# The opening of a 1-core decoder layer: turning x before its norm is known

## The chip, the cores and the metric

The kernel runs on one core of a Trainium2 chip. The metric is the device time in microseconds (us) of one execution. A time is the median of several executions; beside it stands one execution that the hardware profiler recorded, from which all durations of single instructions come.

The engines are called as the profile calls them: PE is TensorE's matrix product and PEld its weight load, DVE is VectorE, ACT is ScalarE, POOL is GpSimd, SP is SyncE, which here only issues DMAs.

## The reference

One layer of a decoder over 512 tokens of width 1024, all in float32. Cut to what the opening of the kernel computes:

```python
def rmsnorm(x, g):
    y = x * rsqrt(mean(x * x, axis=-1) + 1e-6)
    return y * g

u = rmsnorm(x, ln1_g)                 # x [512, 1024]
proj = u @ w_in                       # q, k, v, pool_in, z, xbc, dt, gates
# pooling branch: for each of 4 groups of 256 columns of pool_in, window w in (2, 4, 8, 16)
#   d = (sum of the last w tokens) / min(t + 1, w) - pool_in
#   y_b = concat(d @ pool_w[group]) * pool_scale @ w_b
```

After it come attention of three dilations, a state-space branch, gates, an output projection, a gated convolutional feed-forward block and a final norm. They are not touched.

## The kernel before

**Precision.** A float32 product is made of three products of a shorter format: a matrix a is split into a high part `ah` (rounded to the short format) and a low part `al = a - ah`, and `a @ b` is taken as `ah @ bh + ah @ bl + al @ bh`. For weights, `cast` makes `wh` on ACT (L195) and `lows` makes `wl` on DVE or POOL (L215). For the normed, transposed x the parts lie in `uh` and `ul`, [128, 8, 512]: 128 rows of the width, 8 steps k of it, 512 tokens.

**Jobs.** The work is a list of jobs, each with a block of weights (mostly 1024 x 256, 1 MB) and a body of matrix products. The loop at the end runs the bodies one after the other; before each it issues the low part of the next block, the cast of the one after, and the load of the third. Raw blocks have two buffers. The order on PE, ACT, DVE and POOL is the order in which the program is written (a manual schedule); only SP's queue is not part of it. PSUM has eight banks: four of the tag `mm` for products and four of the tag `sm` for short uses, transposes among them.

**The opening.** The first two jobs (columns 0 to 511 of `pool_in`, pooling groups 0 and 1) are written out by hand ahead of the loop, since the norm of x must be made first. x comes as four blocks of 128 tokens, each in two halves of 512 columns (`xin[tb, h]`). While it loads, PE multiplies ones (`warm_up`, L1493). For blocks 0 and 1 the squares are summed on ACT and DVE, the factor r = 1/sqrt(mean + eps) is made by a chain of short DVE instructions around a square root on ACT, and put on a diagonal matrix `diag`. PE multiplies each 128 x 128 piece of x by `diag` (`turn_scale`, L1552): this transposes and scales at once, into the four `sm` banks, where bank `k % 4` holds the 256 tokens of step k and of step k + 4. `turned` then reads each result, multiplies it by the norm's weight `g1` and splits it: `uh` on ACT (L1522), `ul` on DVE (L1523).

`begin(n, lo, hi)` makes the products of job n for tokens lo to hi into the `mm` banks `first[2n]` and `first[2n+1]` (all L1535): first, interleaved by k, `wh` with `uh` and `ul` (32 products of 256 columns), then `wl` with `uh` (16). The order on PE is

```python
    begin(0, 0, 256)
    begin(1, 0, 256, turns)   # turns: after its first 32 products, transpose blocks 2 and 3
    turn()                    # one transpose of small columns ("colp"), into an sm bank
    begin(0, 256, S)
    begin(1, 256, S)
```

Blocks 2 and 3 are scaled by their factors in place (`xin`, L1587 on DVE and L1589 on ACT), after a chain of its own (`rstd_of`, L421 to L430), and are transposed by plain transposes (L1600). Where all 512 tokens of a bank are done, `pool_evac` copies the bank to `u` (L775) and starts the windowed sums on POOL. The loop's first job is the third block of weights (its products carry L234).

Of the kernel before, what the change touches and what calls it, by code (L numbers as in the profile page):

```python
# [10 lines left out]
F32 = mybir.dt.float32  # L11
# [5 lines left out]
P = 128  # L17
# [66 lines left out]
def trunk(ctx: ExitStack, tc, out, x, rel_bias, ln1_g, w_in, b_gate, w_a, pool_w, pool_scale, w_b,  # L84
# [23 lines left out]
    def T(name, dt=F32, shape=(P, S)):  # L108
        return big.tile(list(shape), dt, name=name, tag="t")
# [76 lines left out]
    def cast(job, cuts=1, spread=False):  # L186

        w = job.c // cuts
        if job.form:
            job.raw = job.form()  # L190
        job.high = whp.tile([P, job.k, job.c], F32R, name="wh", tag="wh")

        def high(i):
            o = slice(i * w, (i + 1) * w)
            act.copy(job.high[:, :, o], job.raw[:, :, o])  # L195
# [12 lines left out]
    def lows(job, cuts=1, eng=None):  # L208

        w, h = job.c // cuts, job.high  # L210
        l = wlp.tile([P, job.k, job.c], F32R, name="wl", tag="wl")
        job.split = h, l
        for i in range(cuts):
            o = slice(i * w, (i + 1) * w)
            (eng or dve).tensor_tensor(l[:, :, o], job.raw[:, :, o], h[:, :, o].bitcast(F32),  # L215
                                       OP.subtract)
# [216 lines left out]
    def squares(eng, src, ss):  # L433
        junk = T("junk")
        if eng is act:
            act.activation(junk, src, AF.Square, accum_out=ss)
        else:
            dve.scalar_tensor_tensor(junk, src, 1.0, src, OP.mult, OP.mult, accum_out=ss)
# [328 lines left out]

    ramp = cpool.tile([P, 4, 16], F32, name="ramp")
    DP, YB = {}, {}

    def pool_evac(m, ps):
        g = m // 2
        w = 2 << g
        u = T("pu")
        act.copy(u, ps)  # L775
        cur, sh = u, 1
        while sh < w:
            nxt = T("psw")
            pool.tensor_tensor(nxt[:, sh:], cur[:, sh:], cur[:, :S - sh], OP.add)
            pool.tensor_copy(nxt[:, :sh], cur[:, :sh])  # L780
            cur, sh = nxt, sh * 2
        pool.tensor_tensor(cur[:, :w], cur[:, :w], ramp[:, g, :w], OP.mult)

        def later():
            yield
            yield
            d = T("pd")
            dve.scalar_tensor_tensor(d, cur, 1.0 / w, u, OP.mult, OP.subtract)
            dh, dl = T("pdh", F32R), T("pdl", F32R)
            act.copy(dh, d)  # L790
            dve.tensor_sub(dl, d, dh.bitcast(F32))
            DP[m] = (dh, dl)

        running.append(later())
# [690 lines left out]
    act.dma_start(g8[:KD, :P], ln1_g[0].rearrange("(k p) -> k p", p=P))  # L1485
    dve.memset(ones, 1.0)
    dve.memset(warm, 1.0)
# [3 lines left out]
    def warm_up(n):  # L1491
        for i in range(n):
            pe.matmul(first[3][:, :P], ones, ones, start=True, stop=True)  # L1493

    fetch(weights[0], 2)
    fetch(weights[1])
    load_x(2)
    load_x(3)
# [17 lines left out]
    def x_block(tb, k):  # L1516
        return xin[tb, k // 4][:, (k % 4) * P:(k % 4 + 1) * P]

    def turned(k, lo, ps):

        hh = uh[:, k, lo:lo + 256]
        act.mul(hh, ps, g1[:, k:k + 1])  # L1522
        dve.scalar_tensor_tensor(ul[:, k, lo:lo + 256], ps, g1[:, k:k + 1], hh.bitcast(F32),  # L1523
                                 OP.mult, OP.subtract)

    def begin(n, lo, hi, between=lambda early: None):
        wh, wl = weights[n].split
        order = [(wh, uh, 0)]
        for k in range(1, KD):
            order += [(wh, uh, k), (wh, ul, k - 1)]  # L1530
        order.append((wh, ul, KD - 1))
        for part in (order, [(wl, uh, k) for k in range(KD)]):
            for a, b, k in part:
                for j in range(2):
                    pe.matmul(first[2 * n + j][:, lo:hi], a[:, k, j * P:(j + 1) * P], b[:, k, lo:hi],  # L1535
                              start=a is wh and b is uh and k == 0, stop=a is wl and k == KD - 1)
            between(part is order)
        if hi == S:
            for j in range(2):
                pool_evac(2 * n + j, first[2 * n + j])  # L1540
                step()


    warm_up(WARM)
    diag = [T("diag") for _ in range(2)]
    banks = [SM("uT") for _ in range(4)]

    def bank(k):
        return banks[k % 4][:, (k // 4) * 256:(k // 4) * 256 + 256]

    def turn_scale(tb, k):
        pe.matmul(bank(k)[:, tb * P:(tb + 1) * P], x_block(tb, k), diag[tb][:, :P], start=True, stop=True)  # L1552

    for tb in range(2):
        s0, s1, v, sq, r, rt = (small(n, [P, 1]) for n in ("s0", "s1", "v", "sq", "r", "rt"))
        squares(act, xin[tb, 0], s0)
        squares((dve, act)[tb], xin[tb, 1], s1)
        dve.tensor_scalar(v, s0, 1.0 / D, EPS, OP.mult, OP.add)
        dve.scalar_tensor_tensor(v, s1, 1.0 / D, v, OP.mult, OP.add)
        act.activation(sq, v, AF.Sqrt)  # L1560
        dve.reciprocal(r, sq)
        dve.scalar_tensor_tensor(rt, r, v, r, OP.mult, OP.mult)
        dve.tensor_scalar(rt, rt, -0.5, 1.5, OP.mult, OP.add)
        dve.tensor_scalar(diag[tb][:, :P], eye, r, rt, OP.mult, OP.mult)
        if tb == 0:
            for k in range(KD):
                turn_scale(0, k)
    pe.transpose(first[2][:, :KD], g8[:KD, :P], eye[:KD, :KD])
    dve.tensor_copy(g1, first[2][:, :KD])
    cast(weights[0], 2)  # L1570
    low(weights[0], 2, pool)
    for k in range(KD):
        turn_scale(1, k % 2 * 4 + k // 2)
    for k in range(KD):
        turned(k, 0, bank(k))
    cast(weights[1], 2)
    parts = lows(weights[1], 2)


    ss = row_squares(2, small("ss", [P, 4]), 2)  # L1580
    next(parts)
    r = rstd_of(ss, 2, D)
    for tb in (2, 3):
        for h in range(2):
            t = xin[tb, h]
            if h:
                dve.tensor_scalar(t, t, r[:, tb - 2:tb - 1], None, OP.mult)  # L1587
            else:
                act.mul(t, t, r[:, tb - 2:tb - 1])  # L1589
    next(parts)  # L1590
    begin(0, 0, 256)

    def turns(early):
        if not early:
            return
        for k in range(4):
            banks[k] = SM("uT")
        for k in range(KD):
            for tb in range(2):
                pe.transpose(bank(k)[:, tb * P:(tb + 1) * P], x_block(2 + tb, k), eye)  # L1600
        for k in range(KD):
            turned(k, 256, bank(k))

    begin(1, 0, 256, turns)
# [6 lines left out]
    begin(1, 256, S)  # L1611
    cast(weights[3])
    fetch(weights[4])

# [68 lines left out]
```

## Time and profile before

| | us |
|---|---|
| median of 3 runs | 1043.03 |
| lowest and highest | 1042.78, 1044.10 |
| the profiled execution | 1044.23 |
| its span, first to last instruction | 1042.4 |

A row of the timeline gives the start and the length in us, the engine, the line, the operation, what it writes and reads, the shape, how many instructions were merged, and in brackets the idle time before with what ended it. A matrix product's length is modelled and overlaps the next one; the distance between starts is what counts. A row of the groups gives the shape, the count, the busy time in us and the mean length of one in ns, and the idle time before. In a row of windows the granted clock of TensorE is a share of full speed.

### The profile page before, as it was taken

The numbers are of one execution on the slowest core, as the hardware profiler recorded it, in microseconds if no ns is written. First come the engines' busy times: TensorE is split into PE (matmuls) and PEld (weight loads), VectorE is DVE, ScalarE is ACT, GpSimd is POOL, SyncE is SP. The second block draws the span as 40 slices with busy tenths as digits, with TensorE's granted clock in tenths as the row PEclk, the third lists the DMA queues.
The fourth block names the chain that finished last, engine by engine and source line by source line (L and its number), as shares of the span: only waits on it lengthen the run. The fifth ranks groups of instructions, "written<-read, shape, count | busy, mean of one in ns | idle before, by whom it ended". The sixth has DMA issues, their size and how long they took to land.

```text
span 1042.4 us, 13096 instructions
## 1 busy us (share of the span) xinstructions
PE 1030.2 (99%) x5214; PEld 864.4 (83%) x5214; DVE 645.8 (62%) x864; ACT 466.9 (45%) x756; POOL 151.1 (14%) x125
## 2 busy tenths in 40 slices
PE   8999999999999999999999999999999999999997
PEld 8988878898888878888888888898888888878885
DVE  5563566684356658766768666767766566556645
ACT  5432554452464364557545233544444344433331
POOL 1680000000000004210152500002111111110110
PEclk9999999999999999999999999999999999999999
DMA  8345222126222344552243326642232322362332
GB/s 294 107 116 148 97 66 75 31 62 201 81 81 81 98 135 112 142 137 80 68 132 122 121 81 242 220 162 86 87 116 81 121 81 97 105 242 70 112 101 81
DMA packets 119788, 121.81 MB, mean 117 GB/s; under 512 B 5523, under 2 KB 101590, under 8 KB 119727
## 3 DMA queue, kind: packets, MB, share of 16 engines
q1 hardware_dynamic: 119135, 120.12, 36.4%
q8 instruction: 41, 0.67, 0.3%
q10 hardware_dynamic: 592, 0.86, 0.2%
q14 instruction: 20, 0.16, 0.1%
HBM read 115.07 MB, written 4.32 MB: 115 GB/s over the span
## 4 chain that ended last, share of the span: by engine, by line
PE 97%; DVE 1%; ACT 1%; DMA 0%; issue 0%; DVEq 0%; SPq 0%; ACTq 0%
PE pa L234 35%; PE pu L234 22%; PE pb L234 17%; PE pqk L234 9%; PE pa L1535 2%; PE p L234 2%; PE ps L662 1%; PE pu L1356 1%; PE ppw L234 1%; PE pt L690 1%; PE po L703 1%; PE py L988 1%; PE uT L1552 1%; PE pyo L995 1%; PE pst L974 0%; DMA xin<-in_x_dram 0%
## 5 line engine op out<-in xcount | busy, mean ns | idle before, releaser
L215 DVE TENSOR_TENSOR wl<-raw,wh 128x2048 fp32r<-128x2048 f32 (+3 forms) x95 | 217.1, 2287 | 73.9 <-ACT wh L195 41.7
L195 ACT CAST wh<-raw 128x1024 fp32r<-128x1024 f32 (+3 forms) x188 | 189.5, 1026 | 63.0 <-DVE raw L337 21.1
L234 PE MATMUL pa<-uh,wh 128*128 128x512 f32 x384 | 98.5, 398 | 0.0
L1192 DVE SCALAR_TENSOR_TENSOR hc<-pu,fcol,hc 128x510 f32<-128x510 f32 x88 | 65.8, 748 | 51.1 <-ACT hc L1189 49.5
L234 PE MATMUL pa<-ul,wh 128*128 128x512 f32 x384 | 94.9, 389 | 0.0
L234 PE MATMUL pa<-uh,wl 128*128 128x512 f32 x384 | 94.9, 389 | 0.0
L234 PEld LDWEIGHTS pa<-ul,wh 128*128 128x128 f32 x384 | 72.1, 188 | 15.2
L234 PEld LDWEIGHTS pa<-uh,wl 128*128 128x128 f32 x384 | 72.1, 188 | 15.0
L234 PE MATMUL pu<-uh,wh 128*128 128x512 f32 (+1 forms) x352 | 83.7, 380 | 0.0
L234 PE MATMUL pu<-ul,wh 128*128 128x512 f32 (+1 forms) x352 | 83.5, 379 | 0.0
L234 PE MATMUL pu<-uh,wl 128*128 128x512 f32 (+1 forms) x352 | 83.5, 379 | 0.0
L234 PEld LDWEIGHTS pa<-uh,wh 128*128 128x128 f32 x384 | 70.3, 188 | 14.7 <-issue 1.0
L234 PEld LDWEIGHTS pu<-uh,wh 128*128 128x128 f32 x352 | 64.1, 188 | 12.6 <-ACT uh L452 0.2
L234 PEld LDWEIGHTS pu<-ul,wh 128*128 128x128 f32 x352 | 64.2, 188 | 12.5
L234 PEld LDWEIGHTS pu<-uh,wl 128*128 128x128 f32 x352 | 64.2, 188 | 12.5
L1189 ACT ACTIVATE hc<-pu,fcol,fcol 128x512 f32<-128x512 f32 x40 | 31.2, 780 | 75.6 <-PE pu L234 75.4
L1197 POOL TENSOR_TENSOR hc<-hc 128x512 f32<-128x512 f32 x22 | 31.5, 1431 | 223.5 <-DVE hc L1192 169.3
L950 POOL TENSOR_TENSOR xd<-xc,dec 128x512 f32<-128x512 f32 x6 | 6.4, 1061 | 333.7 <-DVE xc L944 314.8
L1077 ACT ACTIVATE sg<-pa,col 128x512 f32<-128x512 f32 x24 | 16.5, 688 | 55.5 <-PE pa L234 48.7
L683 ACT ACTIVATE sb<-sb,both 128x128 f32<-128x128 f32 (+1 forms) x72 | 30.1, 419 | 23.5 <-DVE both L680 13.4
L234 PE MATMUL pqk<-uh,wh 128*128 128x512 f32 x144 | 36.9, 394 | 0.0
L234 PE MATMUL pqk<-ul,wh 128*128 128x512 f32 x144 | 36.3, 389 | 0.0
(355 smaller groups left out, 1765.1 us busy)
## 6 DMA issues: line engine op xcount, KB each, us to landing
raw<-in_w_in_dram SPq DMA_DIRECT2D x25, 1024.0 KB
raw<-in_ffn_w_up_dram SPq DMA_DIRECT2D x22, 1024.0 KB
raw<-in_w_in_dram SPq DMA_DIRECT2D x20, 512.0 KB
raw<-in_ffn_w_down_dram SPq DMA_DIRECT2D x10, 1024.0 KB
raw<-in_w_o_dram SPq DMA_DIRECT2D x8, 1024.0 KB
raw<-in_w_b_dram SPq DMA_DIRECT2D x4, 1024.0 KB
al<-ad SPq DMA_DIRECT2D x16, 256.0 KB
raw<-in_w_c_dram SPq DMA_DIRECT2D x4, 1024.0 KB
```

The lines of the kernel that those rows point to most:

```text
L195: act.copy(job.high[:, :, o], job.raw[:, :, o])
L215: (eng or dve).tensor_tensor(l[:, :, o], job.raw[:, :, o], h[:, :, o].bitcast(F32), OP.subtract)
L234: pe.matmul(ps, l, r, start=first and n == 0, stop=last and n == total - 1)
L662: pe.matmul(pss[i][:, o:o + w * P], q[r, n * P:(n + 1) * P], k[r, kb * P:(kb + w) * P], start=True, stop=True)
L683: act.activation(sb[:, off:off + w * P], sb[:, off:off + w * P], AF.Exp, bias=nm[:, n, h:h + 1], accum_out=ls[:, n, h:h + 1])
L690: pe.transpose(pt[:, o:o + P], sb[:, o:o + P], eye)
L703: pe.matmul(po[DH * hh:DH * hh + DH, n * P:(n + 1) * P], V[g, kb + i][:, (2 * cc + hh) * DH:(2 * cc + hh + 1) * DH], probs[2 * cc + hh, mb ...
L1077: act.activation(s, ps, AF.Sigmoid, bias=col[:, o:o + 1])
L1189: act.activation(t, ps, AF.Identity, bias=ff["c1"][:, ff["b"] + m:ff["b"] + m + 1], scale=fw(2, m))
L1192: dve.scalar_tensor_tensor(t[:, sh:], ps[:, :S - sh], fw(k, m), t[:, sh:], OP.mult, OP.add)
L1197: pool.tensor_tensor(a, a, t, OP.mult)
L1535: pe.matmul(first[2 * n + j][:, lo:hi], a[:, k, j * P:(j + 1) * P], b[:, k, lo:hi], start=a is wh and b is uh and k == 0, stop=a is wl and ...
```

## The change

For the first 256 tokens the norm's factor is taken out of the way of the products.

- Blocks 0 and 1 of x are transposed as they are (`turned` is now this transpose), into the same four `sm` banks, `lo`. Between them stand the transpose of the norm's weight and a further warm-up, and another one behind.
- `scaled` multiplies by `g1` and splits into new tiles: `rh` on ACT, `rl` on DVE. Job 0's and job 1's products of these tokens (`highs`, then `lows_of`) run on `rh` and `rl`, with no factor. Since the factor belongs to a token, that is to a column of the result, it is applied to the result: `pool_evac` of the first four banks multiplies the first 256 columns by `rb` on DVE.
- `rb` is the row of factors on all partitions: a diagonal `dg` made on DVE, multiplied by ones on PE (`spread`, in the middle of job 1's high products), copied from the bank by ACT.
- The other jobs still need normed `uh` and `ul` for these tokens. They are made out of the banks: DVE multiplies each `lo[k]` by `g1` and `rb` into `un`; ACT copies that into `uh`, DVE subtracts it into `ul`, during the second half. The chain for blocks 2 and 3 and their scaling stand between the fourth and the fifth of DVE's eight passes. Only then do the `sm` banks take the transposes of blocks 2 and 3.
- Job 0's weights are loaded and split in halves by k instead of by columns; the first half's `wh` is a copy on DVE, the second's a copy on ACT. Job 1's `wl` is made on POOL instead of DVE. The identity matrix `eye` is loaded ahead of block 1 of x.

```diff
     def pool_evac(m, ps):
...
-        act.copy(u, ps)
+        if m < 4:
+            dve.tensor_tensor(u[:, LO], ps[:, LO], rb[0], OP.mult)
+            act.copy(u[:, HI], ps[:, HI])
+        else:
+            act.copy(u, ps)
...
     load_x(0)
+    act.dma_start(eye, c_eye)
     load_x(1, act)
-    act.dma_start(eye, c_eye)
     act.dma_start(g8[:KD, :P], ln1_g[0].rearrange("(k p) -> k p", p=P))
...
-    fetch(weights[0], 2)
+    w0 = weights[0]
+    w0.raw = wraw.tile([P, KD, 256], F32, name="raw", tag="raw")
+    HALF = (slice(0, 4), slice(4, 8))
+    for ks in HALF:
+        sp.dma_start(w0.raw[:, ks, :], w0.parts[0][:, ks, :])
...
+    def scaled(oh, ol, k, ps):
+        act.mul(oh, ps, g1[:, k:k + 1])
+        dve.scalar_tensor_tensor(ol, ps, g1[:, k:k + 1], oh.bitcast(F32), OP.mult, OP.subtract)
+
+    def highs(n, A, B, o, between=None):
+        wh, order = weights[n].split[0], [(A, 0)]
         for k in range(1, KD):
+            order += [(A, k), (B, k - 1)]
+        order.append((B, KD - 1))
+        for i, (m, k) in enumerate(order):
+            if between and i == KD:
+                between()
             for j in range(2):
+                pe.matmul(first[2 * n + j][:, o], wh[:, k, j * P:(j + 1) * P], m(k),
+                          start=m is A and k == 0, stop=False)
+
+    def lows_of(n, A, o):
+        for k in range(KD):
+            for j in range(2):
+                pe.matmul(first[2 * n + j][:, o], weights[n].split[1][:, k, j * P:(j + 1) * P], A(k),
+                          start=False, stop=k == KD - 1)
...
+    def turned(tb, k, ps):
+        pe.transpose(ps[:, tb % 2 * P:(tb % 2 + 1) * P], x_block(tb, k), eye)
...
     warm_up(WARM)
+    lo = banks_of_two()
+    for k in range(KD):
+        turned(0, k, lo[k])
     pe.transpose(first[2][:, :KD], g8[:KD, :P], eye[:KD, :KD])
     dve.tensor_copy(g1, first[2][:, :KD])
+    warm_up(3)
     for k in range(KD):
+        turned(1, k, lo[k])
+    warm_up(6)
+    ss = small("ss", [P, 8])
+    for h in range(2):
+        squares(act, xin[0, h], ss[:, 4 * h:4 * h + 1])
...
+    def split0(ks, copy):
+        copy(w0.high[:, ks, :], w0.raw[:, ks, :])
+        pool.tensor_tensor(wl[:, ks, :], w0.raw[:, ks, :], w0.high[:, ks, :].bitcast(F32), OP.subtract)
+
     for k in range(KD):
+        if k == 1:
+            split0(HALF[0], dve.tensor_copy)
+        if k == 5:
+            split0(HALF[1], act.copy)
+        scaled(rh(k), rl(k), k, lo[k])
+    highs(0, rh, rl, LO)
+    squares(act, xin[1, 0], ss[:, 1:2])
+    squares(dve, xin[1, 1], ss[:, 5:6])
+    dve.tensor_tensor(ss[:, :2], ss[:, :2], ss[:, 4:6], OP.add)
+    r = rstd_of(ss[:, :2], 2, D)
+    dg = T("dg")
+    dve.tensor_tensor(dg[:, LO].rearrange("p (b t) -> p b t", b=2), eye.unsqueeze(1).to_broadcast([P, 2, P]),
+                      r.unsqueeze(2).to_broadcast([P, 2, P]), OP.mult)
+    lows_of(0, rh, LO)
     cast(weights[1], 2)
+    low(weights[1], 2, pool)
+
+    def spread():
+        pe.matmul(first[0][:, HI], ones, dg[:, LO], start=True, stop=True)
+        rb.append(T("rb")[:, :256])
+        act.copy(rb[0], first[0][:, HI])
+
+    ss2 = row_squares(2, small("ss2", [P, 4]), 2)
+    highs(1, rh, rl, LO, spread)
+    us = []
+    for k in range(KD):
+        if k % 2 == 0:
+            us.append(T("un"))
+        t = us[-1][:, k % 2 * 256:k % 2 * 256 + 256]
+        dve.scalar_tensor_tensor(t, lo[k], g1[:, k:k + 1], rb[0], OP.mult, OP.mult)
+        if k == 3:
+            r = rstd_of(ss2, 2, D)
+            for tb in (2, 3):
+                for h in range(2):
+                    t = xin[tb, h]
+                    if h:
+                        dve.tensor_scalar(t, t, r[:, tb - 2:tb - 1], None, OP.mult)
+                    else:
+                        act.mul(t, t, r[:, tb - 2:tb - 1])
+    hi = banks_of_two()
+    for k in range(KD):
+        for tb in (2, 3):
+            turned(tb, k, hi[k])
+    lows_of(1, rh, LO)
+    for k in range(KD):
+        scaled(uhi(k), uli(k), k, hi[k])
+    for i, t in enumerate(us):
+        act.copy(uh[:, 2 * i:2 * i + 2, LO], t.rearrange("p (k t) -> p k t", k=2))
     turn()
     fetch(weights[2])
     fetch(weights[3])
-    begin(0, 256, S)
+    highs(0, uhi, uli, HI)
+    for i, t in enumerate(us):
+        dve.tensor_sub(ul[:, 2 * i:2 * i + 2, LO], t.rearrange("p (k t) -> p k t", k=2),
+                       uh[:, 2 * i:2 * i + 2, LO].bitcast(F32))
+    lows_of(0, uhi, HI)
...
```

More of the change, by code (lines that the diff above doesn't have):

```diff
@@ L769, in trunk @@
     DP, YB = {}, {}
+    rb = []
     def pool_evac(m, ps):
@@ L1517, in x_block @@
         return xin[tb, k // 4][:, (k % 4) * P:(k % 4 + 1) * P]
[L1519 to L1528, printed above, removed]
-        for k in range(1, KD):
[L1530 to L1538, printed above, removed]
-            for j in range(2):
-                pool_evac(2 * n + j, first[2 * n + j])
-                step()
@@ L1544, in trunk @@
-    warm_up(WARM)
[L1545 to L1567, printed above, removed]
+    def scaled(oh, ol, k, ps):
+        act.mul(oh, ps, g1[:, k:k + 1])
+        dve.scalar_tensor_tensor(ol, ps, g1[:, k:k + 1], oh.bitcast(F32), OP.mult, OP.subtract)
@@ new lines, in trunk, with rh, rl, uhi @@
+    raws = [T("rh", F32R) for _ in range(8)]
+    def rh(k):
+        return raws[k // 2][:, k % 2 * 256:k % 2 * 256 + 256]
+    def rl(k):
+        return raws[4 + k // 2][:, k % 2 * 256:k % 2 * 256 + 256]
+    def uhi(k):
+        return uh[:, k, HI]
+    def uli(k):
+        return ul[:, k, HI]
+    def turned(tb, k, ps):
+        pe.transpose(ps[:, tb % 2 * P:(tb % 2 + 1) * P], x_block(tb, k), eye)
+    def banks_of_two():
+        banks = [SM("uT") for _ in range(4)]
+        return [banks[k % 4][:, (k // 4) * 256:(k // 4) * 256 + 256] for k in range(KD)]
@@ L1568, in trunk @@
+    warm_up(WARM)
+    lo = banks_of_two()
+    for k in range(KD):
+        turned(0, k, lo[k])
     pe.transpose(first[2][:, :KD], g8[:KD, :P], eye[:KD, :KD])
     dve.tensor_copy(g1, first[2][:, :KD])
-    cast(weights[0], 2)
-    low(weights[0], 2, pool)
+    warm_up(3)
     for k in range(KD):
-        turn_scale(1, k % 2 * 4 + k // 2)
-    for k in range(KD):
-        turned(k, 0, bank(k))
-    cast(weights[1], 2)
-    parts = lows(weights[1], 2)
-    ss = row_squares(2, small("ss", [P, 4]), 2)
@@ L1581, in trunk @@
[L1581 to L1602, printed above, removed]
@@ L1604, in trunk @@
-    begin(1, 0, 256, turns)
+        turned(1, k, lo[k])
[3 more added lines that the diff above has]
+        squares(act, xin[0, h], ss[:, 4 * h:4 * h + 1])
+    w0.high = whp.tile([P, KD, 256], F32R, name="wh", tag="wh")
+    wl = wlp.tile([P, KD, 256], F32R, name="wl", tag="wl")
+    w0.split = w0.high, wl
+    def split0(ks, copy):
+        copy(w0.high[:, ks, :], w0.raw[:, ks, :])
+        pool.tensor_tensor(wl[:, ks, :], w0.raw[:, ks, :], w0.high[:, ks, :].bitcast(F32), OP.subtract)
@@ L1607, in trunk @@
     fetch(weights[3])
-    begin(0, 256, S)
+    highs(0, uhi, uli, HI)
[3 more added lines that the diff above has]
+    lows_of(0, uhi, HI)
+    for j in range(2):
+        pool_evac(j, first[j])
+        step()
     cast(weights[2])
     low(weights[2])
-    begin(1, 256, S)
+    highs(1, uhi, uli, HI)
+    lows_of(1, uhi, HI)
+    for j in range(2, 4):
+        pool_evac(j, first[j])
+        step()
     cast(weights[3])
```

## The prediction

> **What bounds the kernel now.** I read the page first, then the timeline of TensorE and the chain of work for the first 40 us, the granted clock by windows, and the groups by shape. On the page:
>
> ```profile
> span 1042.4 us, 13096 instructions
> PE 1030.2 (99%) x5214; PEld 864.4 (83%) x5214; DVE 645.8 (62%) x864; ACT 466.9 (45%) x756; POOL 151.1 (14%) x125
> PE 97%; DVE 1%; ACT 1%; DMA 0%; issue 0%; DVEq 0%; SPq 0%; ACTq 0%
> ```
>
> TensorE (PE) is the bound, and 97% of the chain is its own work. So the change is worth what it does to the moment at which TensorE gets through the opening; behind it nothing differs. The opening, from the timeline and (the rows without an engine's instruction form) the chain of work:
>
> ```profile
> 1.05 4.60 PE L1493 MATMUL pa<-ones 128*128 128x128 f32 x24 [1.05 <-DVE relb L515]
> 7.95 3.67 PE L1552 MATMUL uT<-diag,xin 128*128 128x128 f32 x16 [2.30 <-DVE v L1558]
> 11.71 2.05 PE L1552 MATMUL uT<-diag,xin 128*128 128x128 f32 x16
> 13.52 0.72 PE L1535 MATMUL pa<-uh,wh 128*128 128x256 f32 x4
> 23.19 1.91 PE L1600 MATMUL uT<-eye,xin 128*128 128x128 f32 x16
> 24.86 2.15 PE L1535 MATMUL pa<-uh,wl 128*128 128x256 f32 x16
> 38.80 2.00 PE L234 MATMUL pa<-uh,wh 128*128 128x512 f32 x8
> 13.76 9.60 PE pa L1535 x80
> 27.15 0.27 PE colp L503
> 1.18 4.45 DMA xin<-in_x_dram
> ```
>
> After the warm-up TensorE waits 2.30 us for the first norm, then turns block 0 in 3.67 us and block 1 in 2.05 us, although both are 16 instructions. From 13.52 it hardly waits: 80 products in 9.60 us (0.12 each), 16 transposes (0.11 each), 16 products, and so on to the first job of the loop at 38.80. The clock explains the 3.67; the last two rows are of the end of the kernel, where TensorE stops:
>
> ```profile
> 4.55:7.96 3.41, 1.11 (x11) 1.00 1.12 357
> 7.96:11.37 3.41, 3.41 (x16) 0.50 1.10 381
> 11.37:14.79 3.42, 3.42 (x29) 1.00 0.94 341
> 1035.37:1038.79 3.42, 0.26 (x2) 1.00 0.40 154
> 1038.79:1042.30 3.52, 0.00 (x0) 0.50 0.39 149
> ```
>
> (Window, its length, TensorE busy, instructions, clock, DMA.) A stretch of 3.41 us with 1.11 us of work was followed by one at half clock, a full one by full clock, one with 0.26 by half clock. So the change can win the 2.30 us wait and about 1.6 us of slow turning. What it must not do is open a new hole.
>
> **The change, part by part.** *Start of the products.* TensorE turns x itself, so it needs no norm. It leaves the warm-up at 5.65; the second half of block 0 landed at 1.18 + 4.45 = 5.63. Eight transposes at 0.11: 6.5. Then it turns g8, the last load in ACT's queue, now behind the eye and 512 KB of x. What bears on it:
>
> ```profile
> 2.14 0.72 ACTq L1485 DMA_DIRECT2D g<-in_ln_g_dram  x1
> 11.56 0.22 PE L1568 MATMUL pa<-eye,g 8*128 8x8 f32 x1
> 12.46 3.27 ACT L1522 ACTIVATE uh<-uT,g 128x256 fp32r<-128x256 f32 x8 [2.07 <-PE uT L1552]
> 12.96 3.39 DVE L1523 SCALAR_TENSOR_TENSOR ul<-uT,g,uh 128x256 fp32r<-128x256 f32 x8 [0.98 <-ACT uh L1522]
> 8.41 1.98 ACT L195 CAST wh<-raw 128x1024 fp32r<-128x1024 f32 x2
> 9.52 4.68 POOL L215 TENSOR_TENSOR wl<-raw,wh 128x1024 fp32r<-128x1024 f32 x2 [8.56 <-ACT wh L195]
> 24.48 3.02 ACT L1522 ACTIVATE uh<-uT,g 128x256 fp32r<-128x256 f32 x8 [1.52 <-PE uT L1600]
> 24.99 3.23 DVE L1523 SCALAR_TENSOR_TENSOR ul<-uT,g,uh 128x256 fp32r<-128x256 f32 x8 [1.41 <-ACT uh L1522]
> L1587 DVE TENSOR_SCALAR xin<-xin,r 128x512 f32<-128x512 f32 x2 | 0.9, 482 | 0.0
> L215 DVE TENSOR_TENSOR wl<-raw,wh 128x1024 fp32r<-128x1024 f32 x4 | 4.9, 1222 | 15.7 <-PE pb L234 15.7
> ```
>
> The trace only says that g8 was there by 11.56. It may land between 6.5 (TensorE would not notice) and 7.9; I take 6.9, near that 5.63, because only the eye's 64 KB come ahead of x. Then 0.15 for g8, six warm-up instructions (0.67), and block 1 from 7.7 to 8.6; the last warm-up (12 x 0.11) ends at 9.95. ACT may read a bank only when both its halves are turned: before, the first transpose was at 23.19 and ACT's read at 24.48, behind the tenth of 16, so 9 x 0.11 + 0.3. Now it is the fifth: 7.7 + 0.44 + 0.3 = 8.45. ACT's first `rh` takes to 8.9, VectorE's `rl` to 9.4, then VectorE copies half of w0, which no row shows: not under 0.48 (a one-input pass over half the size) nor over 1.22 (two inputs, same size); I take 0.8, nearer to the one-input row. Products start at 10.2 instead of 13.52: **-3.3 us**.
>
> Do they run on? ACT needs 8 x 0.41 plus one cast of 1.0 after 8.45, so 12.7; the last `rh` is wanted at 10.2 + 13 x 0.24 = 13.3: hidden, by 0.6. GpSimd ends `wl` at 10.2 + 4.68 = 14.9; its second half is wanted after 40 products at 15.0: hidden by 0.1, and each tenth beyond costs a tenth. w1's two casts on ACT now stand behind a square root that waits for VectorE:
>
> ```profile
> L436 ACT ACTIVATE junk<-xin 128x512 f32<-128x512 f32 x5 | 3.1, 634 | 0.1
> L438 DVE SCALAR_TENSOR_TENSOR junk<-xin 128x512 f32<-128x512 f32 x3 | 2.0, 687 | 4.6 <-DMA xin<-in_x_dram 4.6
> 18.87 0.16 DVE L1513 TENSOR_TENSOR ss<-ss 128x2 f32<-128x2 f32 x1 [1.30 <-ACT junk L436]
> 18.95 1.22 DVE L215 TENSOR_TENSOR wl<-raw,wh 128x1024 fp32r<-128x1024 f32 x1
> 20.09 0.16 DVE L421 TENSOR_SCALAR v<-ss 128x2 f32<-128x2 f32 x1
> 20.34 0.20 ACT L422 ACTIVATE sq<-v 128x2 f32<-128x2 f32 x1 [1.50 <-DVE v L421]
> 21.37 0.16 DVE L430 TENSOR_TENSOR r<-rt,r 128x2 f32<-128x2 f32 x1
> 21.57 0.88 DVE L1587 TENSOR_SCALAR xin<-xin,r 128x512 f32<-128x512 f32 x2
> 21.63 1.34 ACT L1589 ACTIVATE xin<-xin,r 128x512 f32<-128x512 f32 x2 [1.08 <-DVE r L430]
> L791 DVE TENSOR_TENSOR pdl<-pd,pdh 128x512 fp32r<-128x512 f32 x5 | 4.3, 868 | 4.3 <-ACT pdh L790 4.3
> L775 ACT COPY pu<-pa 128x512 f32<-128x512 f32 x7 | 4.0, 589 | 14.3 <-PE pa L1535 8.5 <-PE pa L234 5.8
> L366 ACT COPY r<-pb 128x384 f32<-128x384 f32 x6 | 2.9, 480 | 8.5 <-PE pb L234 8.3
> ```
>
> VectorE's last `rl` ends about 13.0, its square (0.69) at 13.7, two small steps and the root at 14.2; casts of 1.98 end at 16.15. Tile pair 0 needs 48 x 0.12 on TensorE, to 15.95, and pair 1's second column block wants that cast at 16.1: +0.1.
>
> *The factor row.* Sixteen products into pair 1 (1.92, to 18.0) TensorE spreads the factors over 256 columns: f32, two instructions of twice 0.11, so **+0.44**, to 18.4. ACT copies the row (0.3 until it may read; under the 0.48 of 384 columns, I take 0.4): `rb` at 19.1.
>
> *The hole.* Now VectorE makes normed rows out of the banks: eight passes of L1523's shape, 0.41 each; between the fourth and fifth stand, in its order, the second norm's chain (20.09 to 21.53: 1.44, with ACT's root in it) and two scalings of x (0.88). So passes 0 to 3 end at 20.7, the chain at 22.2, scalings at 23.0, pass 4 at 23.5, pass 7 at 24.7. Queued behind are the split of the second 256 tokens; who waits is TensorE. All four `sm` banks are held by `lo`, and the next transposes need bank 0, read last by pass 4. They need the scaled x too: ACT's part (1.34 for two) is done only at 23.5. TensorE ends pair 1's high products at 16.1 + 3.84 + 0.44 = 20.4 and stands for **3.1 us**. Then banks come free at VectorE's pace: turns at 23.5, 23.9, 24.3, 24.7, then four more k (0.9) without a wait: 25.8, against 24.86 before. So -3.3 + 0.1 + 0.44 + 3.1 + about 0.6 of pacing = **+0.9 us**. What comes next is as late: `colp` needs a bank from VectorE's fifth split, 2.05 after its first (24.99, then 27.15 before); the first is now at 26.0, `colp` at 28.1, again +0.9.
>
> *Costed at nothing.* w1's low halves on GpSimd: 14.9 or the cast, plus 4.68, so under 21, wanted at 25.8; without that cover up to 2.4 a cut. Four `uh` copies on ACT (0.59 each, as L775), four `ul` subtractions (0.87, as L791) and four factor passes in `pool_evac` (0.41) on VectorE, 2.4 and 5.1 us, lie beside the 96 products (11.5 us) of the second half; uncovered, they would delay job 2 (first product at 38.80 before). The squares of blocks 2 and 3 are done on ACT by 17.8, ahead of the factor row.
>
> *The clock.* A hole of 3.1 us plus slow turning leaves between 0.3 and 1.6 us of work in the 3.41 us window that holds it. The trace shows half clock after 1.11 and after 0.26. A half-clock window costs 1.7 us, less what falls in the wait: **+1.4**. Sum: +2.3.
>
> The Trainium skill, page "TensorE: Matmul & The Clock Gate", section "What's actually happening", has the clock fall only after a whole idle window of about 3.4 us. By that rule a hole of 3.1 us never slows it, and the sum stays +0.9; the row with 1.11 us of work speaks against so strict a reading.
>
> The sum stands against the profiled execution (1044.23: span 1042.4 and 1.8 around it), which is 1.2 above the median, 1043.03. Its slow window from 7.96 cost about 1.6; runs without it would be near the median and leave the change less to win. I add a quarter of that 1.2: +2.6 on the median, **1045.6**.
>
> **The rivals.** *The clock stays up*, because the windows cut the hole so that both keep more work than the 1.11 us that was too little: +0.9, so 1043.9, with -0.5 to +2.3 from g8 and the copy. For it: a hole split evenly over two windows leaves 1.8 us of work in each. Against it: such a cut is one of many, and the slow pacing behind the hole thins the second window too. The Trainium skill's rule above would give this case always.
>
> *The second norm does not stand in the way*: VectorE waits for `rb` from about 17.8, where ACT's squares of blocks 2 and 3 end (two of 0.63 and 0.2 from 16.15), to 19.1. If the chain of 1.44 and the 0.88 ran ahead of pass 0, 1.3 of their 2.3 us would fall into that wait; bank 0 would be free at 22.2, the hole 1.8 us, too short for a slow window: +0.9 - 1.3 = -0.4, so 1042.6. This one is not slower, and with g8 at 6.5 (-0.4), a copy of 0.48 (-0.3), and passes and chain a tenth shorter than their rows (-0.5) it reaches -1.6; I let it go to -2.2 for the 0.6 by which runs of before lie on either side of their middle. It decides if the order on VectorE lets the chain pass; against it, before's VectorE runs strictly as written (add at 18.87, `wl` at 18.95, then the chain at 20.09).
>
> *A later start*: g8 at 7.9 and a copy of 1.22 move everything 1.4 later, hole included: +4.0, 1047.0; to 1047.8 with the full clock loss and a late `wl`. For it: g8 is the last of its queue, and TensorE turns it ahead of block 1.
>
> **How the numbers follow.** Hole and slow clock 0.50, clock stays 0.23, chain out of the way 0.15, later start 0.12. A measurement tells about 0.2% (2.1 us) from no change. The first case, +1.0 to +3.6 by its bounds, is slower in 0.41 and same in 0.09; the second 0.03 slower, 0.20 same; the third 0.07 faster (its lower end, and what I have not seen of that kind), 0.08 same; the last 0.11 slower, 0.01 same. Sums: slower 0.55, same 0.38, faster 0.07. The range goes from the third case's lower end, 1040.8, to the last one's upper, 1047.8; the likeliest case alone spans 1044.0 to 1046.6.
>
> **What would show it.** Right: first products near 10.2; TensorE idle about 3 us ahead of the second transposes, ended by VectorE or by the scaled x; 0.50 in the clock within 4 us after; job 2's first product 1 to 2.5 us later than 38.8. Wrong: no hole there; clock 1.00 from 4.6 on; products from before 9.5 or after 11.5.

## The result, and the profile after

The changed kernel takes 1051.37 us (median of 4, 1050.85 to 1052.13) against 1043.38 (median of 4, 1042.78 to 1044.10): a ratio of 1.0077, 95% interval 1.0059 to 1.0094. Slower, as forecast, but by 8.0 us where 2.6 were forecast, and outside the range. The profiled execution took 1052.13. Its page:

```profile
span 1050.3 us, 13130 instructions
PE 1034.6 (99%) x5218; PEld 868.0 (83%) x5218; DVE 657.2 (63%) x875; ACT 467.7 (45%) x759; POOL 155.9 (15%) x127
PE 91%; DVE 4%; ACT 2%; DMA 2%; issue 1%; ACTq 0%; DVEq 0%
```

The span grew by 7.9 us. TensorE's share of the chain that ended last fell from 97% to 91%: VectorE, ACT and a DMA now set the pace somewhere. The timeline of TensorE for the opening says where:

```profile
7.71 0.22 PE L1575 MATMUL pa<-eye,g 8*128 8x8 f32 x1 [0.19 <-DMA g<-in_ln_g_dram]
11.11 4.06 PE L1541 MATMUL pa<-rh,wh 128*128 128x256 f32 x32
18.08 0.38 PE L1541 MATMUL pa<-rh,wh 128*128 128x256 f32 x1 [0.98 <-ACT wh L195]
19.03 2.60 PE L1541 MATMUL pa<-rh,wh 128*128 128x256 f32 x15 [0.56 <-ACT wh L195]
28.81 3.65 PE L1565 MATMUL uT<-eye,xin 128*128 128x128 f32 x16 [3.85 <-ACT xin L1631]
32.11 2.97 PE L1547 MATMUL pa<-rh,wl 128*128 128x256 f32 x16
46.53 1.78 PE L234 MATMUL pa<-uh,wh 128*128 128x512 f32 x7
```

Products start at 11.11 instead of 13.52, job 2 at 46.53 instead of 38.80. From there to the end of the span it is 1003.8 us, before 1003.6: everything happened in the opening. There is a wait ahead of job 1's products, 0.98 + 0.56 us where 0.1 was forecast, and the hole ahead of the second transposes is 3.85 us and ends at 28.81, not at 23.5. The timelines of the engines that TensorE waits for, VectorE first:

```profile
10.88 3.04 DVE L1530 SCALAR_TENSOR_TENSOR rh<-uT,g,rh 128x256 fp32r<-128x256 f32 x7
13.84 2.53 DVE L438 SCALAR_TENSOR_TENSOR junk<-xin 128x512 f32<-128x512 f32 x1
18.11 2.66 DVE L1604 TENSOR_TENSOR dg<-eye,r 128x256 f32<-128x256 f32 x1
20.70 2.84 DVE L438 SCALAR_TENSOR_TENSOR junk<-xin 128x512 f32<-128x512 f32 x1
23.47 0.68 DVE L438 SCALAR_TENSOR_TENSOR junk<-xin 128x512 f32<-128x512 f32 x1
24.34 1.65 DVE L1622 SCALAR_TENSOR_TENSOR un<-uT,g,rb 128x256 f32<-128x256 f32 x4
```

and GpSimd and ACT:

```profile
11.05 4.78 POOL L1590 TENSOR_TENSOR wl<-raw,wh 128x1024 fp32r<-128x1024 f32 x2 [10.09 <-DVE wh L1589]
18.10 4.89 POOL L215 TENSOR_TENSOR wl<-raw,wh 128x1024 fp32r<-128x1024 f32 x2 [2.28 <-ACT wh L195]
17.00 1.98 ACT L195 CAST wh<-raw 128x1024 fp32r<-128x1024 f32 x2
27.45 1.33 ACT L1631 ACTIVATE xin<-xin,r 128x512 f32<-128x512 f32 x2 [1.08 <-DVE r L430]
```

The same square L438 takes 2.53, 2.84 and 0.68 us. The long ones began beside GpSimd. Its first pair of instructions ends at 11.05 + 4.78 = 15.83, the square that began at 13.84 ends at 16.37; the second pair (2.45 us each) ends at about 20.5 and 23.0, `dg` at 20.77 and the next square at 23.54. In each case VectorE ends 0.3 to 0.55 us after a GpSimd instruction. The seven passes L1530 from 10.88 on, which read one operand from a PSUM bank and one from SBUF, run beside GpSimd at their 0.4 us each. The late square delays the root, and behind it in ACT's order stand w1's casts (at 17.00 instead of the forecast 14.2); the late `dg` and second square delay the passes of `un` (24.34 instead of 19.1), the chain for blocks 2 and 3 between them, and with it the scaled x that ends the hole.

The windows of TensorE (start and end, length, TensorE busy and its instructions, granted clock, DMA share, GB/s) show two slow stretches where one was forecast, one window from 20.28 and two from 27.10:

```profile
16.86:20.28 3.42, 1.87 (x13) 1.00 0.83 251
20.28:23.69 3.41, 3.41 (x16) 0.50 1.07 388
23.69:27.10 3.41, 1.27 (x11) 1.00 1.06 397
27.10:30.52 3.42, 1.71 (x8) 0.50 0.55 196
30.52:33.93 3.41, 3.41 (x18) 0.50 0.00 0
```

### The profile page after: what moved, and what is told of

Read it like the earlier page. It is cut to its first block, busy times and chain, and to the rows that moved or that the text cites. A ratio compares the mean times of both kernels' runs of the same rounds, so it can differ in the third digit from the quotient of the medians.

```text
span 1050.3 us, 13130 instructions
## 1 busy us (share of the span) xinstructions
PE 1034.6 (99%) x5218; PEld 868.0 (83%) x5218; DVE 657.2 (63%) x875; ACT 467.7 (45%) x759; POOL 155.9 (15%) x127
## 4 chain that ended last, share of the span: by engine, by line
PE 91%; DVE 4%; ACT 2%; DMA 2%; issue 1%; ACTq 0%; DVEq 0%
PE pa L234 34%; PE pu L234 22%; PE pb L234 15%; PE pqk L234 9%; PE p L234 2%; PE ps L662 1%; DMA raw<-in_ffn_w_up_dram 1%; PE ppw L234 1%; PE pt L690 1%; PE po L703 1%; DVE wl L215 1%; PE py L993 1%; ACT wh L195 1%; PE pa L1541 1%; PE pa L1547 1%; DVE junk L438 1%
## 5 line engine op out<-in xcount | busy, mean ns | idle before, releaser
L215 DVE TENSOR_TENSOR wl<-raw,wh 128x2048 fp32r<-128x2048 f32 (+3 forms) x93 | 214.4, 2306 | 70.3 <-ACT wh L195 34.7
L683 ACT ACTIVATE sb<-sb,both 128x128 f32<-128x128 f32 (+1 forms) x72 | 30.1, 419 | 23.5 <-DVE both L680 13.4
```

The costliest lines, as they stand in the source:

```text
L683: act.activation(sb[:, off:off + w * P], sb[:, off:off + w * P], AF.Exp, bias=nm[:, n, h:h + 1], accum_out=ls[:, n, h:h + 1])
```

## The experiments

Theory A: VectorE's passes with two inputs in SBUF stand while a GpSimd instruction runs, so w0's and w1's low halves on GpSimd push the factor and the second norm back. Theory B: the long rows have another cause, such as the DMA traffic or the half clock. Two further rivals bear on the time: the waits are those of the written order alone, or the slow clock is what costs. The yardstick is the start of three things on TensorE in each timeline: the products, the second transposes, job 2.

| | products | transposes | job 2 | products to transposes | transposes to job 2 |
|---|---|---|---|---|---|
| before | 13.52 | 23.19 | 38.80 | 9.67 | 15.61 |
| after | 11.11 | 28.81 | 46.53 | 17.70 | 17.72 |
| w1's low left out | 13.50 | 28.74 | 46.01 | 15.24 | 17.27 |
| no low on GpSimd | 11.19 | 24.68 | 42.72 | 13.49 | 18.04 |
| the same, clock kept up | 11.48 | 24.97 | 41.12 | 13.49 | 16.15 |
| after, clock kept up | 12.17 | 29.91 | 46.07 | 17.74 | 16.16 |
| short GpSimd instructions | 11.75 | 27.51 | 45.47 | 15.76 | 17.96 |
| before, w1's low on GpSimd | 13.67 | 24.57 | 40.72 | 10.90 | 16.15 |
| factor first | 12.07 | 21.75 | 37.03 | 9.68 | 15.28 |
| weight first | 13.03 | 22.70 | 37.98 | 9.67 | 15.28 |

In the changed kernel and its variants down to the short instructions, the start of the products varies mostly with the landing of g8 (below). The two differences hardly depend on it: with starts 1.06 us apart, the first one is 17.70 and 17.74. Each row is one profiled execution. Each ratio below compares with the kernel before in the same series of runs, whose median was 1042.87 in the first, second, third and fifth experiment and 1043.83 in the others, so medians of different series are not to be subtracted.

**w1's low half left out.** The products that need it take `wh` in its place.

```diff
     cast(weights[1], 2)
-    low(weights[1], 2, pool)
+    weights[1].split = weights[1].high, weights[1].high
```

> Leaves out GpSimd's two passes for the low half of the second weight block (its products take the high half in their place, so the same number of products runs). Theory A, the shared way into memory: a VectorE pass with two inputs in SBUF stands until the GpSimd instruction that runs beside it has ended. Then the diagonal dg takes 0.4 us instead of 2.66 and the square behind it 0.7 instead of 2.84; the first square (2.53) stays, since GpSimd is still at the first weight block there. The factor row still comes at 22.9, so the second transposes start 1.4 us earlier (27.4) and the time is 1048.5 to 1050. Theory B, the stretch has another cause (DMA traffic into SBUF, the half clock): dg and the square stay over 2 us, and the time stays at 1051.

Measured: 1050.02 us, ratio 1.0067 (1.0052 to 1.0082). VectorE's timeline:

```profile
16.12 2.53 DVE L438 SCALAR_TENSOR_TENSOR junk<-xin 128x512 f32<-128x512 f32 x1
20.41 0.42 DVE L1604 TENSOR_TENSOR dg<-eye,r 128x256 f32<-128x256 f32 x1
20.75 0.69 DVE L438 SCALAR_TENSOR_TENSOR junk<-xin 128x512 f32<-128x512 f32 x1
```

The two passes that stood beside w1's low are back at 0.42 and 0.69; the one beside w0's low still takes 2.53. From products to transposes 2.46 us are won. The time shows less of it (a ratio of 1.0067 for 1.0077): in the profiled execution g8 came 1.1 us later and TensorE turned block 1 at half clock, with products at 13.50 and job 2 only 0.52 earlier.

**No low half on GpSimd.** w0's is left out as well, `wh` in its place.

```diff
-    wl = wlp.tile([P, KD, 256], F32R, name="wl", tag="wl")
-    w0.split = w0.high, wl
+    w0.split = w0.high, w0.high
...
-        pool.tensor_tensor(wl[:, ks, :], w0.raw[:, ks, :], w0.high[:, ks, :].bitcast(F32), OP.subtract)
...
-    low(weights[1], 2, pool)
+    weights[1].split = weights[1].high, weights[1].high
```

> Leaves out all four GpSimd passes of the two weight blocks (the products take the high halves in their place). Theory A: all three stretched VectorE passes are back at 0.4 to 0.7; the root comes at 14.7, the second block's casts end at 16.7, TensorE does not stand ahead of pair 1, the factor row is there at 19.9, the second transposes start near 24.4 with a hole of about 3 us ahead of them, as the forecast's own sum had it; the time is 1045 to 1046.7. Theory B: the three passes stay over 2 us and the time within 1 us of 1051.4.

Measured: 1047.08 us, ratio 1.0040 (1.0025 to 1.0055). VectorE and TensorE:

```profile
13.92 0.68 DVE L438 SCALAR_TENSOR_TENSOR junk<-xin 128x512 f32<-128x512 f32 x1
16.35 0.43 DVE L1602 TENSOR_TENSOR dg<-eye,r 128x256 f32<-128x256 f32 x1
16.69 0.69 DVE L438 SCALAR_TENSOR_TENSOR junk<-xin 128x512 f32<-128x512 f32 x1
24.68 3.65 PE L1565 MATMUL uT<-eye,xin 128*128 128x128 f32 x16 [3.02 <-ACT xin L1629]
```

All three passes have their undisturbed lengths, the wait for w1's casts is gone, and 17.70 has become 13.49. So GpSimd's low halves cost 4.21 us up to the transposes: 2.46 by w1's, 1.75 by w0's. A hole of 3.02 us remains, ended by the scaled x. This is the kernel that the prediction had in mind. Its time is 0.4 us above the expected range, and it is still slower than the kernel before.

**The clock kept up in the changed kernel.** Products of ones, 6 and 16, stand in the two waits.

```diff
...
+    keep_busy(6)
     highs(1, rh, rl, LO, spread)
+    keep_busy(16)
```

> Six and sixteen products of ones fill TensorE's two waits, ahead of pair 1 and ahead of the second transposes; nothing else changes. If the half clock is a part of the loss: no 0.50 from 20 to 24 nor from 27 to 34, the second transposes take 1.8 instead of 3.65 and the low products behind them 2.1 instead of 2.97; with the products of 20 to 24 at full speed too, but the same wait for VectorE behind them, 2.7 us at most are won: 1048.5 to 1049.5. If the clock costs nothing that is not hidden: 1051.

Measured: 1051.70 us, ratio 1.0082 (1.0067 to 1.0097); clock 1.00 from 5.88 on. TensorE:

```profile
29.91 2.46 PE L1565 MATMUL uT<-eye,xin 128*128 128x128 f32 x16 [1.84 <-ACT xin L1638]
46.07 1.78 PE L234 MATMUL pa<-uh,wh 128*128 128x512 f32 x7
```

Behind the transposes 1.56 us are won (17.72 to 16.16), ahead of them nothing (17.70 and 17.74): the first slow stretch lay where TensorE had to wait for others anyway. The time did not gain: 1048.5 to 1049.5 was expected, should the clock be a part of the loss. In the profiled execution g8 was late again (products at 12.17, 1.06 later), so job 2 starts only 0.46 earlier, and what follows takes 0.6 us longer (1004.4 us to the end of the span instead of 1003.8), for a reason that the runs do not show. So the slow clock is not the cause of the missing 5 us. Its 1.6 us rest on the rows alone.

**No low half on GpSimd, clock kept up.** The second experiment with 13 such products in the hole.

```diff
     highs(1, rh, rl, LO, spread)
+    keep_busy(13)
```

> As the run without GpSimd's low halves, and the hole ahead of the second transposes filled with 13 products of ones. What is left is the order alone: the hole of 3 us stays as a delay, at full clock. From the products' start (11.2 if the norm's weight lands as before) job 2's first product comes 31.5 - 2.8 = 28.7 us later, at 39.9, 1.1 later than in the kernel before, which is what the forecast's sum without the clock had (+0.9). Time 1044.0 to 1045.0. If the time stays at 1047, the half clock was not what separated that run from the forecast's sum.

Measured: 1046.19 us, ratio 1.0029 (1.0017 to 1.0041). TensorE:

```profile
24.97 2.46 PE L1565 MATMUL uT<-eye,xin 128*128 128x128 f32 x16
41.12 2.00 PE L234 MATMUL pa<-uh,wh 128*128 128x512 f32 x8
```

From the products to job 2 it takes 29.64 us, against 28.7 expected, and the median is 1.2 us above the 1044 to 1045 expected. The clock was expected to be worth 2.8 us and is worth 1.89 (31.53 without the added products), against 1.56 in the changed kernel. With neither GpSimd nor the clock in the way the changed order is still 4.36 us longer than before (25.28): 3.82 up to the transposes and 0.54 behind them. That is what is left to the written order: the factor row, the hole, the pacing.

**GpSimd's low halves in eight short instructions each.**

```diff
-        pool.tensor_tensor(wl[:, ks, :], w0.raw[:, ks, :], w0.high[:, ks, :].bitcast(F32), OP.subtract)
+        for k in range(ks.start, ks.stop):
+            pool.tensor_tensor(wl[:, k, :], w0.raw[:, k, :], w0.high[:, k, :].bitcast(F32), OP.subtract)
...
-    low(weights[1], 2, pool)
+    low(weights[1], 8, pool)
```

> GpSimd's low halves in 8 short instructions for each weight block instead of 2 long ones; the same work. Theory A in its strict form (a VectorE pass waits for the end of the one GpSimd instruction that runs): the three stretched passes wait 0.7 us at most, so 1.3, 1.0 and 1.3 us instead of 2.53, 2.66 and 2.84, and the time is 1046 to 1048.5. If the two engines share the way element by element for as long as GpSimd is busy: the passes stay at 2 us or more and the time at 1050 to 1052. Theory B: no change.

Measured: 1050.42 us, ratio 1.0067 (1.0051 to 1.0084). VectorE, then GpSimd:

```profile
15.28 0.49 DVE L1602 TENSOR_TENSOR ss<-ss 128x2 f32<-128x2 f32 x1
15.81 0.67 DVE L421 TENSOR_SCALAR v<-ss 128x2 f32<-128x2 f32 x1
16.76 0.17 DVE L423 RECIPROCAL r<-sq 128x2 f32<-128x2 f32 x1 [0.27 <-ACT sq L422]
19.30 0.93 DVE L1605 TENSOR_TENSOR dg<-eye,r 128x256 f32<-128x256 f32 x1
20.15 1.22 DVE L438 SCALAR_TENSOR_TENSOR junk<-xin 128x512 f32<-128x512 f32 x1
17.82 6.65 POOL L215 TENSOR_TENSOR wl<-raw,wh 128x256 fp32r<-128x256 f32 x8
```

No pass takes 2.5 us any more: `dg` takes 0.93 and the squares behind it 1.22 and 1.21, each about 0.5 above its undisturbed length, which is less than one short GpSimd instruction. The first square is not hit (0.68); it began together with a GpSimd instruction, and that one took 1.28 us, where the one before it took 0.74. So a VectorE pass gets its turn between two GpSimd instructions and not within one: the wait is as long as what is left of the running instruction. But now nearly every pass is hit, the additions of 128 x 2 numbers too (0.49, alone 0.16). Two inputs are not the whole condition: TENSOR_SCALAR with its one input is hit (0.67, alone 0.17), while the reciprocal with its one input is not (0.17), and what tells the two apart no run here shows. GpSimd needs 6.65 us instead of 4.89. Of the 4.21 us 1.94 come back. The time is a miss, 1046 to 1048.5 was expected: the count of passes that are hit was not in it.

**The kernel before, with w1's low half on GpSimd.** This part of the change by itself.

```diff
-    parts = lows(weights[1], 2)
+    parts = lows(weights[1], 2, pool)
```

> The kernel before, with the low half of its second weight block made on GpSimd instead of VectorE. Theory A: of the two squares on VectorE near 16.3 and 16.9 the second meets GpSimd's first pass (about 16.7 to 19.1) and takes 2.6 us instead of 0.69, and the scaling of x near 21 waits for the end of the second pass (21.4). TensorE wants the turned x only at 23.1, so the time stays within 1 us of the kernel before. Theory B: the squares keep 0.69.

Measured: 1045.03 us, ratio 1.0019 (1.0009 to 1.0029). VectorE, GpSimd and TensorE:

```profile
17.04 2.89 DVE L438 SCALAR_TENSOR_TENSOR junk<-xin 128x512 f32<-128x512 f32 x1
20.04 2.17 DVE L1513 TENSOR_TENSOR ss<-ss 128x2 f32<-128x2 f32 x1
16.90 5.28 POOL L215 TENSOR_TENSOR wl<-raw,wh 128x1024 fp32r<-128x1024 f32 x2 [2.58 <-ACT wh L195]
24.57 0.33 PE L1600 MATMUL uT<-eye,xin 128*128 128x128 f32 x1 [1.06 <-ACT xin L1589]
```

An addition of two numbers per partition takes 2.17 us where it took 0.16, and the square 2.89. No change within 1 us was expected, and that was a miss: TensorE waits 1.06 us for the scaled x, and the time rises by 0.19%. In a kernel whose order is otherwise the old one, this single move costs.

**The order mended: the factor first.** All four squares of blocks 0 and 1 on ACT as they land; the factor's chain and `dg` ahead of the first split; the factor row spread ahead of job 0's products; the eight `un` passes right behind the splits; then the norm of blocks 2 and 3; w1's low half on VectorE again; `colp` later. The last warm-up is shortened from 6 to 4, and blocks 2 and 3 are scaled one on ACT and one on VectorE, instead of half by half. Several things change at once here, so this run shows that the order can be mended, not what each part is worth.

```diff
+    for b in range(2):
+        for h in range(2):
+            squares(act, xin[b, h], ss[:, 4 * h + b:4 * h + b + 1])
+    dve.tensor_tensor(ss[:, :2], ss[:, :2], ss[:, 4:6], OP.add)
+    r = rstd_of(ss[:, :2], 2, D)
...
+    pe.matmul(first[2][:, LO], ones, dg[:, LO], start=True, stop=True)
     highs(0, rh, rl, LO)
...
+    rb.append(T("rb")[:, :256])
+    act.copy(rb[0], first[2][:, LO])
+    us = [T("un") for _ in range(4)]
+    for i in range(KD):
+        k = i % 2 * 4 + i // 2
+        dve.scalar_tensor_tensor(us[k // 2][:, k % 2 * 256:k % 2 * 256 + 256], lo[k], g1[:, k:k + 1], rb[0],
+                                 OP.mult, OP.mult)
     lows_of(0, rh, LO)
     cast(weights[1], 2)
-    low(weights[1], 2, pool)
...
```

> The change with its order mended: the squares of block 1 on ACT right behind block 0's, factor and diagonal made before the first split, the factor row spread ahead of pair 0's products, the eight passes that free the banks right behind the splits (13.9 to 17.2), the second norm behind them, the second block's low half on VectorE in two halves by k, the small columns' transpose later. No VectorE pass with two SBUF inputs but the first low halves' time meets GpSimd. If theory A and the order are the whole loss: no hole ahead of the second transposes, full clock, job 2 near 36.4 instead of 38.8, time 1040.5 to 1041.5. If something else in the opening costs (the load of the norm's weight, banks), it stands between 1043 and 1047.

Measured: 1042.30 us, ratio 0.9991 (0.9982 to 1.0000). TensorE, then the last square of block 1 on ACT:

```profile
8.36 0.22 PE L1575 MATMUL pa<-eye,g 8*128 8x8 f32 x1 [1.18 <-DMA g<-in_ln_g_dram]
12.07 4.06 PE L1541 MATMUL pa<-rh,wh 128*128 128x256 f32 x32 [0.39 <-ACT rh L1529]
21.75 1.91 PE L1565 MATMUL uT<-eye,xin 128*128 128x128 f32 x16
37.03 2.00 PE L234 MATMUL pa<-uh,wh 128*128 128x512 f32 x8
8.12 0.63 ACT L436 ACTIVATE junk<-xin 128x512 f32<-128x512 f32 x1 [0.30 <-DMA xin<-in_x_dram]
```

No hole, the clock at 1.00 from 5.94 on, 9.68 us from products to transposes, as before (9.67). GpSimd still makes w0's low half (12.00 to 16.79), but the VectorE passes beside it read one operand from a PSUM bank, and they take 0.40 us each. So turning x before its norm need not cost anything between products and transposes; what cost was GpSimd's share and the order. Job 2 starts 1.77 us earlier than before, and the time is 0.09% lower by the ratio, with an interval that reaches 1.0000. It is the best kernel of the study, level with the one before or slightly faster; 1040.5 to 1041.5 and job 2 near 36.4 were expected. TensorE still waits 1.18 us for g8.

**The same, with g8 loaded ahead of block 1.**

```diff
     act.dma_start(eye, c_eye)
-    load_x(1, act)
     act.dma_start(g8[:KD, :P], ln1_g[0].rearrange("(k p) -> k p", p=P))
+    load_x(1, act)
```

> As the mended order, and the norm's weight (4 KB) loaded ahead of block 1 of x instead of behind it. In the runs so far it landed between 7.7 and 8.8, and TensorE stood up to 1.8 us for it. If that wait is on the path: products start 0.8 to 1.5 us earlier than in the mended order, 1039.5 to 1040.5. If block 1's own landing (about 7) or the split sets the start: no difference.

Measured: 1043.69 us, ratio 1.0007 (0.9997 to 1.0016). TensorE, then ACT:

```profile
9.10 0.66 PE L1565 MATMUL uT<-eye,xin 128*128 128x128 f32 x4 [0.79 <-DMA xin<-in_x_dram]
13.03 4.07 PE L1541 MATMUL pa<-rh,wh 128*128 128x256 f32 x32 [0.39 <-DVE wh L1595]
9.07 0.63 ACT L436 ACTIVATE junk<-xin 128x512 f32<-128x512 f32 x1 [0.72 <-DMA xin<-in_x_dram]
```

A miss: 1039.5 to 1040.5 was expected. The wait for g8 is gone, but block 1's second half now comes later, its squares and the factor with it, and products start at 13.03. In both mended kernels products start 3.95 us behind the start of block 1's last square (12.07 and 8.12, 13.03 and 9.07): with the factor's chain ahead of the first split, it is block 1's landing and that chain that set the start, and the wait for g8 was not what had to be won. The medians of the two, ten runs each, are 1.4 us apart, so the later landing is not a matter of one execution; why so small a load moves the block by that much stays open.

## Why the prediction was right in direction and wrong in size

The difference in job 2's start, 7.73 us, by the table, beside the terms of the prediction's sum:

| term | forecast | measured | from |
|---|---|---|---|
| earlier products | -3.3 | -2.41 | 11.11 - 13.52 |
| order: casts, factor row, hole | 0.1 + 0.44 + 3.1 | +3.82 | 13.49 - 9.67 |
| GpSimd's low halves | 0 | +4.21 | 17.70 - 13.49 |
| pacing behind the transposes | 0.6 | +0.55 | 16.16 - 15.61 |
| slow clock | 1.4 | +1.56 | 17.72 - 16.16 |

**The step that failed** is in the part headed "Costed at nothing": "w1's low halves on GpSimd: 14.9 or the cast, plus 4.68, so under 21, wanted at 25.8". It asked only whether GpSimd would be in time. It was (22.99 in the changed kernel, wanted at 32.11); what it did meanwhile to VectorE was not asked, and a term of 4.21 us stood at nothing. The same omission is in "its square (0.69) at 13.7", beside w0's low half, which the prediction itself had running to 14.9. Both took durations from rows of undisturbed passes. And "the squares of blocks 2 and 3 are done on ACT" is half of it: two of the four stand on VectorE, and one of those is the pass of 2.84 us. Without GpSimd's low halves the two take 0.69 each and lie in VectorE's wait for `rb` (16.69 to 17.99, `un` from 20.20), so there they cost nothing.

The direction was not luck: with GpSimd's low halves left out the kernel is still slower (ratio 1.0040), by the order and the clock, as the prediction has it. Only that part of the 8.0 us was foreseen.

The profile of before could have told. In its timelines the same pass L788, with two inputs in SBUF, takes 0.68 us in one place and 1.50 in another, where GpSimd starts just ahead of it (VectorE, VectorE, GpSimd):

```profile
46.57 0.68 DVE L788 SCALAR_TENSOR_TENSOR pd<-psw,pu 128x512 f32<-128x512 f32 x1
49.06 1.50 DVE L788 SCALAR_TENSOR_TENSOR pd<-psw,pu 128x512 f32<-128x512 f32 x1 [0.36 <-POOL psw L782]
48.98 1.04 POOL L779 TENSOR_TENSOR psw<-pu 128x511 f32<-128x511 f32 x1
```

The wait ends where GpSimd's instruction ends (48.98 + 1.04 = 50.02), and 0.54 later the pass is done. The Trainium skill, page "SBUF — State Buffer", section "SBUF: two separate sides", states just this: VectorE and GpSimd hold a shared pair of ports exclusively, whoever comes first keeps it for the whole instruction and the other stands, and a VectorE pass with two SBUF inputs is such a case beside a GpSimd instruction that reads SBUF. For passes with two inputs in SBUF the runs here agree (2.53, 2.66, 2.84, 2.89 and 2.17 us beside GpSimd; 0.68, 0.42, 0.69, 0.69 and 0.16 without); the TENSOR_SCALAR of 0.67 us, with its one input, is not such a case. It was the rule that spoke against this change, and the prediction did not weigh it.

**The products' start** was mis-sized by 0.9: g8 landed at 7.66 where I took 6.9 (the bound was 7.9), and block 1 was turned from 8.63, not 7.7. The copy of half of w0 on VectorE, bounded by 0.48 and 1.22 and taken as 0.8, took 0.68.

**The hole** was right as a mechanism and, without GpSimd, in size: 3.1 forecast, 3.02 measured with the low halves left out, ended by the scaled x on ACT as the prediction had it. In the changed kernel it is 3.85, since the norm's chain starts later still. Had the prediction's own sum been right, job 2 would have started 2.3 us later than before; without GpSimd's low halves it starts 3.92 later. The rest, 1.6 us, is 1.0 by the products' start, 0.2 by the order and 0.5 by the clock, less 0.1 of pacing. The three rivals did not happen: the clock fell, the second norm did stand in the way, and the start was late by 0.9 rather than 1.4.

**The clock** fell behind the hole as forecast, and its 1.56 us are near the 1.4 of the sum. The nearness is in part luck: one slow window was in the sum, and there were two, the first (27.10) mostly a wait; without GpSimd's low halves the clock is worth 1.89. That it fell once more, at 20.28, was not forecast and cost nothing, as the run with the clock kept up in the changed kernel shows (17.70 and 17.74). The Trainium skill's rule, page "TensorE: Matmul & The Clock Gate", section "What's actually happening", by which only a whole idle window lowers it, does not hold here: windows with 1.87 and 1.27 us of work were followed by 0.50.

**The squares, copies and subtractions** that were costed at nothing in the second half cost next to nothing: with the clock kept up, 16.16 us from the transposes to job 2 against 15.61 leave 0.55 for everything, and the 16 transposes alone take 2.46 instead of 1.91, which is the forecast pacing.

## What to carry to other kernels

Work moved to GpSimd is not free just because GpSimd is idle: list the VectorE passes that run meanwhile, and count each that reads two operands from SBUF (here TENSOR_SCALAR too) as ending only after the GpSimd instruction then running. Look in the trace for one line with two very different durations before taking its mean. And where a factor is applied late so that products can start early, whatever needs the factor next (here the banks' second reading) wants its chain ahead of everything else on VectorE, or the wait only moves.

## What the runs showed of the hardware that was not expected

- It goes the other way too, as the Trainium skill, page "SBUF — State Buffer", section "SBUF: two separate sides", has it. In the changed kernel's timelines a GpSimd copy of one number per partition (line 785) takes 2.25 us when VectorE's L215 has started just before, and ends with it; the same copy 1.4 us earlier, at 42.74, takes 0.19:

```profile
44.14 2.25 POOL L785 COPY psw<-pu 128x1 f32<-128x1 f32 x1
43.91 2.44 DVE L215 TENSOR_TENSOR wl<-raw,wh 128x2048 fp32r<-128x2048 f32 x1 [2.31 <-POOL psw L787]
```

- How little work lowers the clock is not decided by its amount alone. Windows of 3.41 us with 1.87 us (after) and 1.64 us (w1's low left out) of work were followed by half clock, one with 1.71 was not; this is the window behind which, in the changed kernel with the clock kept up, the clock stayed at 1.00:

```profile
26.36:29.77 3.41, 1.71 (x16) 1.00 1.02 371
```

- The last small load of a queue is a poor thing to wait for: TensorE turned g8 at 7.71, 7.78, 8.07, 8.34, 8.36, 8.76 and 8.80 in seven kernels whose loads ahead of it are the same, one profiled execution each. That spread of 1.1 us is not small beside the effects studied here (0.55 to 4.21), which is why the table goes by differences from the products' start.
